# Weight sums through idle x places, and gate weights in 12 tiles per pair of blocks

## The chip, the cores and the metric

The kernel runs on one NeuronCore of a Trainium2 chip. A core has five engines with an instruction queue each: TensorE (PE; its weight loads are shown apart as PEld), VectorE (DVE), ScalarE (ACT), GpSimd (POOL) and SyncE (SP). SyncE issues nearly all loads, GpSimd nearly all stores; the transfers themselves run on 16 DMA engines. Every queue is worked off in order: an instruction that waits holds all those behind it. The metric is the time of one execution on the device in microseconds.

## The reference, cut to what matters

A decoder trunk of two layers over 2048 tokens of width 1024, fp32:

```python
# layer 0: x = x + mlstm_mixer(rmsnorm(x))
proj = u @ w_in                      # xm, z, o: 2048 columns each, and i, f: 4 each
xc = silu(causal_dwconv(xm))
q, k, v = per head from xc, xc, xm
h = chunkwise mLSTM, 64 tokens a chunk
y = (norm(sigmoid(o) * h) + skip * xc) * silu(z)
return y @ w_out                     # w_out: 2048 x 1024
# layer 1: x = x + rglru_mixer(rmsnorm(x))
proj = u @ w_in                      # xr, g: 1536 columns each
xc = causal_dwconv(xr)
xb = xc.reshape(bsz, s, 8, 192)      # 8 blocks of 192 channels
r  = sigmoid(xb @ w_a + b_a)         # per block 192 x 192
ig = sigmoid(xb @ w_x + b_x)
log_a = -8 * r * softplus(-lam)
bt = sqrt(-expm1(2 * log_a)) * (ig * xc)
hs = scan over tokens: h = exp(log_a) * h + bt
return (hs * silu(g)) @ w_out        # 1536 x 1024
# and a final rmsnorm
```

The two things the change touches are `y @ w_out` of layer 0 (its weights are prepared long before it is computed) and the two gate products `xb @ w_a`, `xb @ w_x` of layer 1.

## The kernel before, in words

Activations lie with channels on the 128 partitions and tokens along the free axis, in blocks of 512 tokens. Every fp32 product is made of three matmuls: each operand is split into a rounded high part (a ScalarE cast, L750) and the rest (a VectorE subtraction, L753), and `mm3` (L359 to L361) adds high × high, low × high and high × low into one PSUM bank. There are eight banks of 128 x 512.

**Phases.** a1: first norm and the projections xm, z, o; a2: chunkwise mLSTM; b: the output projection `y @ w_out`, second norm, the projections xr and g; b2: gates, scan, output projection of layer 1, final norm.

**Phase a1.** Large products go by a seven-product scheme on 2 x 2 quarters (a "group": seven products of 12 matmuls on sums of quarters, whose partial results pa, pb, pc, pd VectorE adds up at L271). Tokens are worked in two slabs of 1024, s = 0 and 1. In each slab come first six groups whose first product was made early (`first`, these are z outputs; "late groups" below), then 14 or so middle items: four "q" items (`o_group`, the o projection of a head; they begin with the copies `G<-oa`, L540) and the groups of the other outputs. Weights of a group stream from DRAM: in the second slab the raw quarters come over SyncE (L83, L424) and their stored sums come back into the s ring (`s<-d_wx`, L98).

**The weight sums of phase b.** `wout_sums(k)`, k = 0 to 7, loads four 128 x 512 pieces of w_out (L468) into four places of the x ring, makes four combinations in place (L471), splits each into a slot of the s ring of 128 x 1024 (cast `s<-x` L750, low part L753) and stores the slot with one DMA of 512 KB on GpSimd's queue (L93, `d_ws<-s`). Phase b reads these sums back. The program calls it at the first eight middle items of the second slab. The x ring has eight places, the s ring eight slots, which the streaming weights use too. The x ring held the input blocks of the first slab and is not otherwise used by the second slab's middle items.

**Phase b2.** For each block b of 512 tokens and each pair p = 0 to 3 of gate blocks (a pair is 384 channels, three partition tiles xc[0..2]) the generator `gates` runs in two halves. The weights of a pair are cut into 128 x 128 tiles: output tile 0 needs input tiles 0, 1; output tile 1, in which the border of the two blocks lies, needs 0, 1, 2; output tile 2 needs 1, 2: seven tiles for r and seven for ig. Half 0 makes r: tanh (L1425), exp to A (L1428), tanh to R (L1429), then one square root over all three tiles (L1433, which changes ScalarE's function table) and a VectorE product (L1436). Half 1 makes ig (tanh, L1431), then on VectorE the products (L1438, L1439), the scan (L1442), the product with silu(g) (L1445), and the split into yh and yl, which the matmuls `acc<-yh,wr` of the output projection need. The steps of gates ("g") and of the output projection ("r") are interleaved in `steps` with a lag of five, so that matmuls of one block's output projection lie between gate halves of the next.

**What sets the order.** The program text gives each instruction a place, but a list scheduler of the compiler decides the order on each engine from its own estimate of when operands and buffers are free; so instructions may move far ahead of the place of their call.

Of the kernel before, what the change touches and what calls it, by code (L numbers as in the profile page):

```python
# [8 lines left out]
F32R = mybir.dt.float32r  # L9
I32 = mybir.dt.int32  # L10
AF = mybir.ActivationFunctionType
# [3 lines left out]
P = 128  # L15
# [291 lines left out]
class Trunk:  # L307
# [74 lines left out]
    def phase_a1(self, xT, woq, wxz, wout, D):  # L382
        tc, nc = self.tc, self.nc
        with ExitStack() as ctx:
# [77 lines left out]

            def wout_sums(k):

                A = {}
                for nm, kk, c in (("11", k, 0), ("21", k, 512), ("22", k + 8, 512), ("12", k + 8, 0)):
                    A[nm] = S.x()
                    nc.sync.dma_start(A[nm], wout[kk, :, c:c + 512])  # L468

                def comb(out, a, b, op):  # L470
                    nc.vector.tensor_tensor(A[out], A[a], A[b], op=op)  # L471
                comb("22", "21", "22", ALU.add)
                comb("21", "11", "21", ALU.subtract)
                comb("11", "22", "11", ALU.subtract)
                comb("12", "12", "11", ALU.subtract)
                for nm, i in (("22", 0), ("11", 1), ("21", 2), ("12", 3)):
                    S.split(A[nm], D["ws"][i, k])

# [133 lines left out]
            for k in range(KD):  # L612
                S.scale(xs, None, pb, (k,))
                nm = ("u11", "u21")[k // 4]
                U[nm, k % 4] = S.operand(nm, k % 4, xs[k], "v")
            ew = []
            for s in range(2):
                t = []
# [11 lines left out]
                for j, (kind, i) in enumerate(middle):  # L630
                    W = stream()
                    if s == 1 and j < 8:
                        wout_sums(j)
                    if kind == "q":
# [689 lines left out]
    def phase_b2(self, rgate, rwout, D, outT):  # L1324
# [4 lines left out]
        with ExitStack() as ctx:  # L1329
# [14 lines left out]
            def fetch(kind, b, i):  # L1344

                m = 896 if kind == "g" else 512
                pool = gp if kind == "g" else wp
                keep = D["gw" if kind == "g" else "ow"][i]
                if b > 0:
# [3 lines left out]
                raw = pool.tile([P, m], F32, tag="wr" + kind, name="wr", bufs=2)  # L1353
                nc.gpsimd.dma_start(raw, rgate[i // 2, :, i % 2 * 896:(i % 2 + 1) * 896] if kind == "g" else
                                    rwout[i % NT, :, i // NT * 512:(i // NT + 1) * 512])
# [52 lines left out]
            def gates(b, p, xs, ys):  # L1408
# [4 lines left out]
                xc, xh, xl = xs  # L1413
                for j in range(2):
                    wh, wl = weights()
                    i = 0
                    for to, tis in ((0, (0, 1)), (1, (0, 1, 2)), (2, (1, 2))):
                        ps = psum("gate")
                        for ti in tis:
                            ws = slice(i * P, (i + 1) * P)  # L1420
                            self.mm3(ps, wh[:, ws], wl[:, ws], xh[:, ti], xl[:, ti], ti == tis[0], ti == tis[-1])
                            i += 1
                        t = p * 3 + to
                        if j == 0:
                            a = nc.scalar.activation(R[:, to], ps, AF.Tanh, scale=0.5, bias=col(2, t))  # L1425
                            if b == 0 and t == 5:
                                self.first.append(a)
                            nc.scalar.activation(A[:, to], R[:, to], AF.Exp, scale=col(0, t), bias=col(0, t))  # L1428
                            nc.scalar.activation(R[:, to], R[:, to], AF.Tanh, scale=col(1, t), bias=col(1, t))  # L1429
                        else:  # L1430
                            nc.scalar.activation(G[:, to], ps, AF.Tanh, scale=0.5, bias=col(3, t))  # L1431
                    if j == 0:
                        nc.scalar.activation(R, R, AF.Sqrt, scale=-0.25)  # L1433
                        g = tp.tile([P, 3, TB], F32, tag="g", name="g")
                        nc.sync.dma_start(g, D["g"][p * 3:p * 3 + 3, :, b * TB:(b + 1) * TB].rearrange("k p t -> p k t"))
                        nc.vector.scalar_tensor_tensor(R, A, 1.0, R, op0=ALU.add, op1=ALU.mult)  # L1436
                        yield
                nc.vector.scalar_tensor_tensor(xc, G, 1.0, xc, op0=ALU.add, op1=ALU.mult)  # L1438
# [94 lines left out]
def host(inputs):  # L1533
# [36 lines left out]
    o["rwout"] = np.ascontiguousarray(f["r_w_out"][0].reshape(12, P, DM))  # L1570
    rg = np.zeros((4, P, 14, P), np.float32)
    for p in range(4):
        i = 0
        for nm in ("r_w_a", "r_w_x"):
            m = np.zeros((384, 384), np.float32)
            m[:192, :192] = f[nm][0][2 * p]
            m[192:, 192:] = f[nm][0][2 * p + 1]
            for to, tis in ((0, (0, 1)), (1, (0, 1, 2)), (2, (1, 2))):
                for ti in tis:
                    rg[p, :, i] = m[ti * P:(ti + 1) * P, to * P:(to + 1) * P]  # L1580
                    i += 1
    o["rgate"] = rg.reshape(4, P, 1792)
    o["gbias"] = np.stack([np.repeat(f["m_b_i"][0], 16), np.repeat(f["m_b_f"][0], 16)], axis=1)
# [3 lines left out]
def trunk_kernel(tc, xT, woq, wxz, wq, wk, wv, wout, rwin, rgate, rwout, vecs, gbias, outT):  # L1587
    with ExitStack() as ctx:
        K = Trunk(ctx, tc, vecs, gbias)
        D = {}  # L1590
        for n, shape in (("o", [NTC, P, MI]), ("xm", [16, P, T]), ("xc", [16, P, T]), ("sz", [16, P, T]),
                         ("y", [16, P, T]), ("x1", [KD, P, T]), ("xr", [12, P, T]), ("g", [12, P, T]), ("q", [64, P]), ("dec", [64, P]), ("wx", [16, 4, P, 1024]),
                         ("wq", [H, 4, 2, P, 1032]), ("wr", [12, 4, P, 1024]), ("ws", [4, 8, P, 1024]),
                         ("gw", [8, P, 1792]), ("ow", [24, P, 1024])):
            D[n] = tc.dram_tile(shape, F32, name="d_" + n)
# [28 lines left out]
```

## Time and profile before

| | us |
|---|---|
| median of three runs | 3014.07 (3010.29 to 3014.26) |
| profiled execution | 3012.88, span 3011.1, mean TensorE clock 0.983 |
| TensorE busy | 2886.6 (96%) |
| VectorE, ScalarE, GpSimd busy | 2128.8, 1496.0, 433.1 |

The late groups of the second slab lie at 548 to 632 us, its middle items with the weight sums at 632 to about 900, phase b2 from about 2520 to the end. The page gives sums over the whole span; for what one change is worth, the windows and waits of its own stage are read. In a row of a timeline the first number is the start, the second the duration, and a bracket at the end names the idle time ahead of it and who ended it. In a row of a tile the three numbers behind the count are the shortest, median and longest duration in ns (for DMA issues: the issue alone), then the first and last start; "landing" is the time from issue to arrival.

### The profile page before, as it was taken

The page shows a single profiled execution, that of the slowest core. Times are in us where ns is not written, and L with a number is a line of the kernel's source. Part 1 is how long each engine was busy: PE and PEld are TensorE (multiplying, and loading weights), DVE is VectorE, ACT ScalarE, POOL GpSimd, SP SyncE. Part 2 cuts the span into 40 slices and gives each one's busy share as a digit, 9 for nine tenths or more (in the row PEclk, how much of TensorE's full clock was granted, in tenths as well). Part 3 has the DMA queues.
Part 4 walks back from the last instruction along what each step waited for, and adds up shares of the span by engine and source line. Part 5 has one row for each costly group of instructions (what it writes and reads, how often), then busy time and mean ns, then how long its engine had stood idle before and what let it go on. Part 6 is the DMA issues. An engine that isn't in the chain of part 4 may idle for free. (4 is left out here: it accounts for less than half of the span.)

```text
span 3011.1 us, 43310 instructions
## 1 busy us (share of the span) xinstructions
PE 2886.6 (96%) x15538; PEld 2469.6 (82%) x15538; DVE 2128.8 (71%) x3596; ACT 1496.0 (50%) x2526; POOL 433.1 (14%) x838
## 2 busy tenths in 40 slices
PE   7999999999899999999999899999999998899997
PEld 5799987898887799998999777887888886687886
DVE  7766788535567588788888756768889475766654
ACT  6344555324334466666666433435445235865651
POOL 1211132101112111111111201002221111110000
PEclk9999999999999999999999999999999998999998
DMA  6767677768887745444443667676766657878865
GB/s 227 266 220 252 229 250 244 244 206 293 282 275 262 224 138 168 130 147 153 146 146 121 246 220 269 217 246 219 244 230 212 217 177 279 297 268 291 295 201 185
DMA packets 289272, 672.43 MB, mean 223 GB/s; under 512 B 28064, under 2 KB 106656, under 8 KB 289056
## 3 DMA queue, kind: packets, MB, share of 16 engines
q1 hardware_dynamic: 219952, 425.17, 44.7%
q0 software_dynamic: 68528, 243.44, 21.2%
q8 instruction: 122, 2.00, 0.3%
q10 hardware_dynamic: 576, 1.05, 0.1%
q14 instruction: 94, 0.77, 0.1%
HBM read 431.33 MB, written 238.22 MB: 222 GB/s over the span
## 5 line engine op out<-in xcount | busy, mean ns | idle before, releaser
L750 ACT CAST s<-raw 128x512 fp32r<-128x512 f32 (+1 forms) x280 | 171.6, 620 | 246.3 <-PE pd L361 71.5
L753 DVE TENSOR_TENSOR s<-raw,s 128x512 fp32r<-128x512 f32 (+1 forms) x280 | 191.7, 689 | 69.3 <-ACT s L750 68.2
L359 PE MATMUL acc<-yh,wr 128*128 128x512 f32 x384 | 153.7, 407 | 17.4 <-ACT yh L750 11.4
L360 PE MATMUL acc<-yl,wr 128*128 128x512 f32 x384 | 155.1, 404 | 1.7 <-DVE yl L753 1.7
L361 PE MATMUL acc<-yh,wr 128*128 128x512 f32 x384 | 154.4, 402 | 0.0
L750 ACT CAST u<-t 128x512 fp32r<-128x512 f32 x112 | 68.8, 619 | 153.1 <-PE pc L361 50.3
L677 DVE SCALAR_TENSOR_TENSOR xc<-xm,vec,xc 128x512 f32<-128x512 f32 x192 | 139.4, 747 | 5.4 <-ACT xc L675 4.2
L753 DVE TENSOR_TENSOR u<-t,u 128x512 fp32r<-128x512 f32 x112 | 76.8, 690 | 84.2 <-ACT u L750 83.8
L750 ACT CAST s<-sum 128x512 fp32r<-128x512 f32 (+1 forms) x120 | 74.0, 618 | 116.8 <-PE pc L361 46.5
L359 PE MATMUL pa<-u,s 128*128 128x512 f32 x304 | 122.5, 403 | 4.6 <-ACT p L258 3.1
L360 PE MATMUL pa<-u,s 128*128 128x512 f32 x304 | 121.6, 400 | 0.0
L361 PE MATMUL pa<-u,s 128*128 128x512 f32 x304 | 121.4, 400 | 0.1
L750 ACT CAST Ch<-C 128x516 fp32r<-128x516 f32 x120 | 74.8, 623 | 85.4 <-DVE da L980 70.3
L962 DVE SCALAR_TENSOR_TENSOR C<-C,dl,kv 128x516 f32<-128x516 f32 x112 | 83.7, 747 | 47.2 <-PE kv L361 47.2
L677 DVE SCALAR_TENSOR_TENSOR xc<-xr,vec,xc 128x512 f32<-128x512 f32 x144 | 106.0, 748 | 9.2 <-ACT xc L675 8.1
L359 PEld LDWEIGHTS acc<-yh,wr 128*128 128x128 f32 x384 | 73.7, 193 | 38.9 <-ACT yh L750 13.6
L359 PE MATMUL pj<-vwh,xmh 128*128 128x512 f32 x256 | 102.7, 402 | 0.7 <-ACT vwh L750 0.7
L360 PE MATMUL pj<-vwl,xmh 128*128 128x512 f32 x256 | 99.9, 390 | 0.8 <-DVE vwl L753 0.8
L753 DVE TENSOR_TENSOR s<-sum,s 128x512 fp32r<-128x512 f32 (+1 forms) x120 | 82.7, 690 | 24.9 <-ACT s L750 24.1
L361 PE MATMUL pj<-vwh,xml 128*128 128x512 f32 x256 | 100.2, 391 | 0.0
L359 PE MATMUL gate<-xch,wg 128*128 128x512 f32 x224 | 90.6, 406 | 9.4 <-ACT xch L750 9.3
L360 PEld LDWEIGHTS acc<-yl,wr 128*128 128x128 f32 x384 | 74.3, 193 | 20.8 <-DVE yl L753 3.4
(481 smaller groups left out, 10090.9 us busy)
## 6 DMA issues: line engine op xcount, KB each, us to landing
wr<-d_ow SPq DMA_DIRECT2D x72, 512.0 KB, 3.7
d_wx<-s POOLq DMA_DIRECT2D x64, 512.0 KB, 4.3
s<-d_wx SPq DMA_DIRECT2D x64, 512.0 KB, 4.8
s<-d_ws SPq DMA_DIRECT2D x64, 512.0 KB, 6.5
raw<-in_wxz_dram SPq DMA_DIRECT2D x124, 256.0 KB, 4.7
d_wr<-s POOLq DMA_DIRECT2D x48, 512.0 KB, 3.7
s<-d_wr SPq DMA_DIRECT2D x48, 512.0 KB, 4.2
raw<-in_rwin_dram SPq DMA_DIRECT2D x94, 256.0 KB, 3.8
```

The source lines that it names most:

```text
L359: mm(out, sh, mh, start=first, stop=False, skip_group_check=resumed)
L360: mm(out, sh, ml, start=False, stop=False, skip_group_check=resumed)
L361: mm(out, sl, mh, start=False, stop=last, skip_group_check=resumed)
L677: nc.vector.scalar_tensor_tensor(out, x[:, j:j + TB], self.v(wn, m * 4 + j), out, op0=ALU.mult, op1=ALU.add)
L750: a = nc.scalar.copy(hi, src)
L753: b = (nc.gpsimd if lo_eng == "p" else nc.vector).tensor_tensor(lo, src, hi.bitcast(F32), op=ALU.subtract)
L962: nc.vector.scalar_tensor_tensor(C2, C2, self.dl[:, r:r + 1], p2, op0=ALU.mult, op1=ALU.add)
```

## The change

It has two parts.

**Weight sums.** `wout_sums` is cut in two: `wout_blocks(k)` takes four x places and loads the pieces; `wout_sums(k, A)` makes the same combinations, takes a further x place for the high part of each and leaves the low part in place, and stores the two parts with a DMA of 256 KB each. No s slot is used. The calls stand at the middle items 0, 2, 3, 5, 7, 8, 10, 11, and a sum is made one item behind its loads.

**Gates.** For output tile 1 the program now packs columns: its first 64 columns belong to the first block of the pair and need input tiles 0, 1; its last 64 belong to the second and need 1, 2. The bank "low" holds 64 columns of r and 64 of ig over tiles 0, 1, and "high" the same over tiles 1, 2, with the halves swapped. So a pair has six output banks of two tiles each, 12 tiles, in place of six banks of 2, 3 and 2. Half 0 makes r0, low and high, half 1 makes r2, i0 and i2; the activations of the shared banks work on 64 partitions each (four in place of two), and the square root with its product stands in half 1, since r2 is made there. The weights of one half are 768 columns wide (896 before).

```diff
-            def wout_sums(k):
+            def wout_blocks(k):
 
                 A = {}
                 for nm, kk, c in (("11", k, 0), ("21", k, 512), ("22", k + 8, 512), ("12", k + 8, 0)):
                     A[nm] = S.x()
                     nc.sync.dma_start(A[nm], wout[kk, :, c:c + 512])
+                return A
+
+            def wout_sums(k, A):
 
                 def comb(out, a, b, op):
                     nc.vector.tensor_tensor(A[out], A[a], A[b], op=op)
...
                 for nm, i in (("22", 0), ("11", 1), ("21", 2), ("12", 3)):
-                    S.split(A[nm], D["ws"][i, k])
+                    hi, lo = S.x(), A[nm]
+                    self.split_into(hi.bitcast(F32R), lo.bitcast(F32R), lo, "a", "v")
+                    nc.gpsimd.dma_start(D["ws"][i, k, :, 0:TB], hi)
+                    nc.gpsimd.dma_start(D["ws"][i, k, :, TB:2 * TB], lo)
...
+            spread, sums = (0, 2, 3, 5, 7, 8, 10, 11), []
...
                     W = stream()
-                    if s == 1 and j < 8:
-                        wout_sums(j)
+                    if sums:
+                        wout_sums(*sums.pop())
+                    if s == 1 and j in spread:
+                        sums.append((spread.index(j), wout_blocks(spread.index(j))))
...
-                m = 896 if kind == "g" else 512
+                m = 768 if kind == "g" else 512
...
-                for j in range(2):
+                def banks(what):
                     wh, wl = weights()
                     i = 0
-                    for to, tis in ((0, (0, 1)), (1, (0, 1, 2)), (2, (1, 2))):
+                    for nm, tis in what:
                         ps = psum("gate")
                         for ti in tis:
                             ws = slice(i * P, (i + 1) * P)
                             self.mm3(ps, wh[:, ws], wl[:, ws], xh[:, ti], xl[:, ti], ti == tis[0], ti == tis[-1])
                             i += 1
-                        t = p * 3 + to
-                        if j == 0:
-                            a = nc.scalar.activation(R[:, to], ps, AF.Tanh, scale=0.5, bias=col(2, t))
...
-                            nc.scalar.activation(A[:, to], R[:, to], AF.Exp, scale=col(0, t), bias=col(0, t))
-                            nc.scalar.activation(R[:, to], R[:, to], AF.Tanh, scale=col(1, t), bias=col(1, t))
-                        else:
-                            nc.scalar.activation(G[:, to], ps, AF.Tanh, scale=0.5, bias=col(3, t))
-                    if j == 0:
+                        yield nm, ps
...
+                for nm, ps in banks((("r0", (0, 1)), ("low", (0, 1)), ("high", (1, 2)))):
+                    if nm == "r0":
+                        rec(0, ps, every)
+                        rates(0)
+                    elif nm == "low":
+                        rec(1, ps, low)
+                        inp(1, ps, low, high)
+                    else:
+                        rec(1, ps, high)
+                        inp(1, ps, high, low)
+                        rates(1)
+                yield
+                for nm, ps in banks((("r2", (1, 2)), ("i0", (0, 1)), ("i2", (1, 2)))):
+                    if nm == "r2":
+                        a = rec(2, ps, every)
...
+                        rates(2)
                         nc.scalar.activation(R, R, AF.Sqrt, scale=-0.25)
                         g = tp.tile([P, 3, TB], F32, tag="g", name="g")
                         nc.sync.dma_start(g, D["g"][p * 3:p * 3 + 3, :, b * TB:(b + 1) * TB].rearrange("k p t -> p k t"))
                         nc.vector.scalar_tensor_tensor(R, A, 1.0, R, op0=ALU.add, op1=ALU.mult)
-                        yield
+                    else:
+                        inp(int(nm[1]), ps, every, every)
```

Lines of the changed program have other numbers: the combinations are L474 (L471 before), splits L759 and L762 (L750, L753), the half stores L482 and L483, the square root L1463 (L1433), tanh of r L1435 (L1425), tanh of ig L1438 (L1431), exp and tanh of the rates L1442 and L1443 (L1428, L1429).

VectorE, phase a1, second slab, at the end of the first late group and through the second (z, u and p are the groups' work tiles, pb to pd their PSUM banks, raw and s the streamed weights). Before:

```order
L271 TENSOR_TENSOR z<-pd,u_5638 128x512
L271 TENSOR_TENSOR u_5729<-pb,p_5300 128x512
L753 TENSOR_TENSOR s<-raw,s 128x512
L271 TENSOR_TENSOR p_5300<-pc,u_5729 128x512
L271 TENSOR_TENSOR z<-pd,p_5300 128x512
L271 TENSOR_TENSOR z<-pc,u_5729 128x512
L271 TENSOR_TENSOR z<-pd,u_5729 128x512
```

and after:

```order
L271 TENSOR_TENSOR z<-pd,u_5638 128x512
L474 TENSOR_TENSOR x<-x 128x512 x2
L271 TENSOR_TENSOR u_5729<-pb,p_5300 128x512
L762 TENSOR_TENSOR s<-raw,s 128x512
L474 TENSOR_TENSOR x<-x 128x512 x2
L271 TENSOR_TENSOR p_5300<-pc,u_5729 128x512
L762 TENSOR_TENSOR x<-x 128x512 x3
L271 TENSOR_TENSOR z<-pd,p_5300 128x512
L762 TENSOR_TENSOR x<-x 128x512
L271 TENSOR_TENSOR z<-pc,u_5729 128x512
L474 TENSOR_TENSOR x<-x 128x512
L271 TENSOR_TENSOR z<-pd,u_5729 128x512
```

Sum 1 now stands in the second late group. It is so in all six: of the eight sums all 32 combinations and low parts stand ahead of the first `G<-oa` of the middle items, the last two combinations of sum 7 just behind and the two before them just ahead of the last addition of the sixth group. Before, only the combinations of sums 0 and 1 stood there.

SyncE, the same groups. Before:

```order
L98 DMA s<-d_wx 128x1024 x3
L424 DMA raw<-in_woq_dram 128x516
L98 DMA s<-d_wx 128x1024 x4
L424 DMA raw<-in_woq_dram 128x516
L98 DMA s<-d_wx 128x1024 x4
L83 DMA raw<-in_wxz_dram 128x512
```

and after:

```order
L98 DMA s<-d_wx 128x1024
L468 DMA x<-in_wout_dram 128x512
L98 DMA s<-d_wx 128x1024
L468 DMA x<-in_wout_dram 128x512 x2
L98 DMA s<-d_wx 128x1024
L468 DMA x<-in_wout_dram 128x512
L98 DMA s<-d_wx 128x1024
L468 DMA x<-in_wout_dram 128x512
L424 DMA raw<-in_woq_dram 128x516
L98 DMA s<-d_wx 128x1024
L468 DMA x<-in_wout_dram 128x512 x2
L98 DMA s<-d_wx 128x1024
```

Loads of w_out now stand between the loads of the stored weight sums; each of them takes an x place whose store must have landed.

ScalarE, phase b2, from the last rate steps of a pair to the cast of the next pair's input. Before:

```order
L1425 ACTIVATE R<-gate,lc 128x512
L1429 ACTIVATE R<-R,lc 128x512
L1428 ACTIVATE A<-R,lc 128x512
L1429 ACTIVATE R<-R,lc 128x512
L1433 ACT_TABLE_LOAD
L1433 ACTIVATE R<-R 128x1536
L1511 COPY rb<-srow 128x512
L1431 ACT_TABLE_LOAD
L1431 ACTIVATE ig<-gate,lc 128x512 x3
L750 CAST xch<-xc 128x1536
```

and after:

```order
L1435 ACTIVATE R<-gate,lc 128x512
L1442 ACTIVATE A<-R,lc 128x512
L1438 ACTIVATE ig<-gate,lc 128x512
L1443 ACTIVATE R<-R,lc 128x512
L1438 ACTIVATE ig<-gate,lc 128x512
L1463 ACT_TABLE_LOAD
L1463 ACTIVATE R<-R 128x1536
L759 CAST xch<-xc 128x1536
L1435 ACT_TABLE_LOAD
```

The square root has moved behind the last tanh of ig. On TensorE the matmuls between the last gate matmul of pair 3 and the first output matmul on that pair's yh number 64 between blocks (57 before), as ten gate matmuls of the next block's second half are drawn ahead, and 37 behind the last block (36 before). The gate matmuls are 576 in all (672 before).

More of the change, by code (lines that the diff above doesn't have):

```diff
@@ L1353, in fetch @@
                 raw = pool.tile([P, m], F32, tag="wr" + kind, name="wr", bufs=2)
-                nc.gpsimd.dma_start(raw, rgate[i // 2, :, i % 2 * 896:(i % 2 + 1) * 896] if kind == "g" else
+                nc.gpsimd.dma_start(raw, rgate[i // 2, :, i % 2 * 768:(i % 2 + 1) * 768] if kind == "g" else
                                     rwout[i % NT, :, i // NT * 512:(i // NT + 1) * 512])
@@ L1422, in gates, with rec, inp, rates @@
                             i += 1
-                        t = p * 3 + to
-                        if j == 0:
[L1425 to L1428, printed above, removed]
-                            nc.scalar.activation(R[:, to], R[:, to], AF.Tanh, scale=col(1, t), bias=col(1, t))
-                        else:
-                            nc.scalar.activation(G[:, to], ps, AF.Tanh, scale=0.5, bias=col(3, t))
-                    if j == 0:
+                        yield nm, ps
+                def rec(to, ps, rows):
+                    return nc.scalar.activation(R[rows, to], ps[rows], AF.Tanh, scale=0.5, bias=col(2, p * 3 + to)[rows])
+                def inp(to, ps, rows, src):
+                    nc.scalar.activation(G[rows, to], ps[src], AF.Tanh, scale=0.5, bias=col(3, p * 3 + to)[rows])
+                def rates(to):
+                    t = p * 3 + to
+                    nc.scalar.activation(A[:, to], R[:, to], AF.Exp, scale=col(0, t), bias=col(0, t))
+                    nc.scalar.activation(R[:, to], R[:, to], AF.Tanh, scale=col(1, t), bias=col(1, t))
+                every, low, high = slice(0, P), slice(0, 64), slice(64, P)
+                for nm, ps in banks((("r0", (0, 1)), ("low", (0, 1)), ("high", (1, 2)))):
[13 more added lines that the diff above has]
+                        a = rec(2, ps, every)
+                        if b == 0 and p == 1:
+                            self.first.append(a)
+                        rates(2)
                         nc.scalar.activation(R, R, AF.Sqrt, scale=-0.25)
@@ L1570, in host @@
     o["rwout"] = np.ascontiguousarray(f["r_w_out"][0].reshape(12, P, DM))
-    rg = np.zeros((4, P, 14, P), np.float32)
+    rg = np.zeros((4, P, 12, P), np.float32)
     for p in range(4):
-        i = 0
[L1574 to L1582, printed above, removed]
+        m = []
+        for nm in ("r_w_a", "r_w_x"):
+            m.append(np.zeros((384, 384), np.float32))
+            m[-1][:192, :192] = f[nm][0][2 * p]
+            m[-1][192:, 192:] = f[nm][0][2 * p + 1]
+        r, x = m
+        low = np.concatenate([r[:, 128:192], x[:, 128:192]], axis=1)
+        high = np.concatenate([x[:, 192:256], r[:, 192:256]], axis=1)
+        i = 0
+        for w, tis in ((r[:, 0:128], (0, 1)), (low, (0, 1)), (high, (1, 2)), (r[:, 256:384], (1, 2)),
+                       (x[:, 0:128], (0, 1)), (x[:, 256:384], (1, 2))):
+            for ti in tis:
+                rg[p, :, i] = w[ti * P:(ti + 1) * P]
+                i += 1
+    o["rgate"] = rg.reshape(4, P, 1536)
     o["gbias"] = np.stack([np.repeat(f["m_b_i"][0], 16), np.repeat(f["m_b_f"][0], 16)], axis=1)
@@ L1593, in trunk_kernel @@
                          ("wq", [H, 4, 2, P, 1032]), ("wr", [12, 4, P, 1024]), ("ws", [4, 8, P, 1024]),
-                         ("gw", [8, P, 1792]), ("ow", [24, P, 1024])):
+                         ("gw", [8, P, 1536]), ("ow", [24, P, 1024])):
             D[n] = tc.dram_tile(shape, F32, name="d_" + n)
```

## The prediction

> **What bounds the kernel now.** I read the page first, then stage by stage the table of windows, and after it the waits, tiles and timelines of the two places the change touches.
>
> ```profile
> span 3011.1 us, 43310 instructions
> PE 2886.6 (96%) x15538; PEld 2469.6 (82%) x15538; DVE 2128.8 (71%) x3596; ACT 1496.0 (50%) x2526; POOL 433.1 (14%) x838
> ```
>
> TensorE is busy for 96% of the span: 124.5 us of 3011.1 are idle. A change gains by taking matmuls away where TensorE is the bound, or by closing one of its gaps; it loses wherever it makes a new one. The columns of the next view are the window, its length, the busy time of TensorE, weight loads, VectorE, ScalarE and GpSimd with their instruction counts, the granted clock, the DMA share and GB/s.
>
> ```profile
> core 0: us, PE busy (x) PEld busy (x) DVE busy (x) ACT busy (x) POOL busy (x), PEclk, DMA share, GB/s
> 150.00:310.00 160.00, 160.00 (x1168) 152.00 (x1167) 107.23 (x239) 76.31 (x143) 27.32 (x51) 1.00 0.66 231
> 548.00:632.00 84.00, 84.00 (x364) 67.94 (x363) 34.61 (x53) 17.94 (x29) 10.25 (x19) 1.00 0.74 241
> 690.00:900.00 210.00, 193.70 (x1289) 176.54 (x1290) 122.20 (x273) 81.96 (x153) 27.89 (x52) 0.98 0.84 285
> 2520.00:2627.00 107.00, 86.57 (x327) 66.21 (x327) 75.39 (x63) 89.41 (x114) 24.15 (x45) 0.89 0.92 332
> 2627.00:2740.00 113.00, 109.58 (x459) 88.07 (x460) 77.77 (x72) 69.01 (x90) 16.12 (x29) 0.96 0.81 287
> 2860.00:2900.00 40.00, 40.00 (x174) 32.52 (x173) 25.27 (x17) 20.60 (x26) 0.00 (x0) 1.00 0.63 211
> ```
>
> Rows 1 and 3 hold the same kind of work, the middle items of phase a1, without and with the weight sums. With them TensorE is idle for 210.00 − 193.70 = 16.3 us and the clock is 0.98; without them it has neither. Row 2 is the stretch just ahead, the six late groups of the second slab: no idle at all. Row 4 is block 0 of the gate phase, with 20.4 us of idle; row 6 a steady piece of it, full, where 40.00 / 174 = 0.230 us is the price of one 512-column matmul.
>
> **The middle items, 690 to 900 us.** The sums are removed from here: the order of VectorE puts all eight ahead of the first middle item, although the program text spreads their calls. The waits of TensorE here (us in all, times, longest) and what the sums do:
>
> ```profile
> PE pd L359 <- DVE xm L271: 7.2, 3, 3.3
> PE st L714 <- DVE gate L709: 2.6, 1, 2.6
> PE st L694 <- DVE G L540: 1.1, 1, 1.1
> ```
> ```profile
> L468 SPq DMA_DIRECT2D x<-in_wout_dram x32: 327/333/1185, 543.2 to 872.1; - x32
> L471 DVE TENSOR_TENSOR x<-x x32: 681/687/695, 553.0 to 877.9; 128x512 f32<-128x512 f32 x32
> L750 ACT CAST s<-x x32: 601/620/622, 672.3 to 903.5; 128x512 fp32r<-128x512 f32 x32
> L753 DVE TENSOR_TENSOR s<-x,s x32: 620/692/694, 672.9 to 904.2; 128x512 fp32r<-128x512 f32 x32
> DMA to landing us min/median/max: 3.1/5.3/7.4
> ```
>
> The longest waits are for VectorE, whose queue holds sums that themselves wait for loads. What can go is the 16.3 us of idle and the lost clock, 0.02 × 210 = 4.2 us: 20.5 in all. The two gate steps (2.6 + 1.1 us) have nothing to do with the sums. I take **−16** (bounds −20.5, and −12 if some clock loss stays). Row 1 is the cover: the same items ran there with no gap.
>
> **The late groups, 548 to 632 us.** What left the middle arrives here. Before, only the combinations of sums 0 and 1 stood here; now all 32 combinations, 32 casts on ScalarE, 32 low parts on VectorE, and 64 stores of 256 KB on GpSimd's queue (32 of 512 KB before), whose issues are short. The engines have room: 24 × 0.687 + 32 × 0.692 = 38.6 us more on VectorE, beside 34.6 busy of 84. The question is the wait. A sum takes four x places for its blocks and four for the high parts, all eight of the ring, so the loads of the next sum wait until the stores of this one have landed; and the additions of the groups (L271) stand behind the combinations in VectorE's queue, TensorE's PSUM banks behind those additions, and the next groups' weight loads (s<-d_wx) behind the waiting x loads in SyncE's queue. The prices:
>
> ```profile
> 553.02 1.41 DVE L471 TENSOR_TENSOR x<-x 128x512 f32<-128x512 f32 x2
> 559.20 2.13 DVE L471 TENSOR_TENSOR x<-x 128x512 f32<-128x512 f32 x3
> 632.05 0.69 DVE L271 TENSOR_TENSOR z<-pd,u 128x512 f32<-128x512 f32 x1 [2.10 <-PE pd L361]
> 639.27 0.16 DVE L540 COPY G<-oa 128x2 f32<-128x2 f32 x1
> ```
> ```profile
> GB/s 193 238 125 198 339 218 198 294 390 402 358 243 221 0 81 94 239 153 254 322 340 398 279 239 190 301 209 193 269 235 174 249 277 175 120 202 197 207 299 54
> s<-d_wx SPq DMA_DIRECT2D x24, 512.0 KB, 4.2
> d_sz<-z POOLq DMA_DIRECT2D x32, 256.0 KB, 4.0
> x<-in_wout_dram SPq DMA_DIRECT2D x8, 256.0 KB, 6.1
> ```
> ```profile
> d_ws<-s POOLq DMA_DIRECT2D x29, 512.0 KB, 5.5
> ```
> ```profile
> L93 POOL DMA_DIRECT2D d_ws<-s x32: 531/532/539, 673.9 to 905.2; - x32
> DMA to landing us min/median/max: 2.9/6.1/10.9
> ```
>
> One round: three combinations 2.1 (the x3 row), two casts 1.2, the store's issue 0.5 and landing 4.0 (d_sz, the same size, 460 to 640 us) to 5.5 (d_ws, 640 to 900 us), the next load's issue 0.3 and landing 5.3: C = 13.4 to 14.9 us. Sum 0 starts at 553.0 as before; the combinations of sum 7 stand ahead of the last addition of group 6, which therefore can't come before 553.0 + 7C = 647 to 657 instead of 632.05: +15 to +25. With the shortest landings of the rows, 2.9 and 3.1, C is 10.1 and nothing is lost. With 6.1 for both landings (the whole d_ws tile and the x loads of this stretch) C is 16.3: +35.
>
> A second way, by bytes: the stretch moves 241 × 84 = 20.2 MB; eight sums are 64 × 256 KB of stores and 32 × 256 KB of loads, 25.2 MB, of which eight loads (2.1) were there already: 43.3 MB. At 402 GB/s, the fullest slice of the DMA view (460 to 640 us), that is 107.7 us, or 97.3 if the last two sums' stores (4.2 MB) land later: +13 to +24. At what row 4 of the windows would make of a full share, 332 / 0.92 = 361 GB/s, it is 108 to 120 us: +24 to +36. Both ways meet between 15 and 25; I take **+22**, bounds 0 and +36.
>
> The Trainium skill, page "DMA: Bandwidth & Descriptors", section "Anatomy of one DMA — SWDGE (gpsimd) path", prices a store as about 2.0 us plus its bytes at 436 GB/s; for 256 KB that is an estimate of 2.6 us, and with it for both landings a round would take 9.3 us and the sums would keep pace (rival 2). The rows above, 4.0 to 6.1 us, are longer, so I go by them. The same page's section "Where 436 GB/s comes from" sets about 358 GB/s as a core's share of HBM; that speaks against this change and would put the loss at +25 to +37, though the 402 of one slice shows that this rate is passed at times.
>
> **The gates (phase b2).** Each pair of blocks drops 2 of 14 tiles: 2 × 3 matmuls, 96 over 16 pairs. Each pair gains two ScalarE activations, since the shared banks are read by halves of 64 rows.
>
> ```profile
> L1425 ACT ACTIVATE R<-gate,lc x48: 663/672/695, 2527.0 to 2926.0; 128x512 f32<-128x512 f32 x48
> L1431 ACT ACTIVATE ig<-gate,lc x48: 667/687/691, 2538.0 to 2939.3; 128x512 f32<-128x512 f32 x48
> L701 ACT ACTIVATE gate<-gate x1: 312/312/312, 873.7 to 873.7; 64x128 f32<-64x128 f32 x1
> ```
> ```profile
> PE acc L359 <- ACT yh L750: 11.4, 4, 3.3
> ```
>
> An activation on 64 rows of 512 columns isn't in the trace. A 64x128 one took 0.312; four times the columns cost at most 4 × 0.312 = 1.25 and at least that 0.31. I take 0.67, the same columns on twice the rows: 32 × 0.67 = 21.4 us more on ScalarE (10 to 40). In blocks 1 to 3 this lies beside matmuls: ScalarE is busy 69.01 of 113 in row 5 and 20.60 of 40 in row 6.
>
> Blocks 1 to 3 lose 72 matmuls: 72 × 0.230 = −16.6, as TensorE is nearly full there. In block 0 ScalarE is busy 89.41 of 107 us and TensorE isn't the bound: 24 matmuls could give −5.5, eight more activations could cost +5.4; I take 0.
>
> The square root (L1433, with its table load) and the product behind it move from the first half of a pair to the second, so they come after the last gate matmul:
>
> ```profile
> 2823.57 1.76 DVE L1436 SCALAR_TENSOR_TENSOR R<-A,R 128x1536 f32<-128x1536 f32 x1 [6.57 <-ACT R L1433]
> 2834.94 1.75 DVE L1439 TENSOR_TENSOR R<-R,xc 128x1536 f32<-128x1536 f32 x1
> 2836.73 3.63 DVE L1442 TENSOR_TENSOR_SCAN xc<-A,hcarry,R 128x512 f32<-128x512 f32 x3
> 2840.40 1.76 DVE L1445 TENSOR_TENSOR g<-xc,g 128x1536 f32<-128x1536 f32 x1
> ```
> ```profile
> 2820.76 1.28 ACT L1433 ACT_TABLE_LOAD   x1
> 2822.05 1.49 ACT L1433 ACTIVATE R<-R 128x1536 f32<-128x1536 f32 x1
> 2842.19 1.48 ACT L750 CAST yh<-g 128x1536 fp32r<-128x1536 f32 x1 [1.01 <-DVE g L1445]
> ```
> ```profile
> L1428 ACT ACTIVATE A<-R,lc 128x512 f32<-128x512 f32 x5 | 4.0, 805 | 0.0
> ```
>
> From the last gate matmul to yh it is now tanh 0.69, table 1.28, root 1.49, product 1.76, product 1.75, scan 3.63, product 1.76 and cast 1.48: 13.8 us. The cover between blocks is 64 matmuls in the changed order (57 before), 64 × 0.230 = 14.7 us: just enough, so 0 there. Behind the last pair of block 3 only 37 matmuls stand, 8.5 us: a wait of 5.3 instead of the longest in the row above, 3.3: +2 (0 to +4). Gates: −16.6 + 0 + 2 = **−15** (bounds −22, all 96 matmuls and no new wait, and −4, worked out as rival 3).
>
> **Sum.** −16 + 22 − 15 = −9 us against the profiled execution's 3012.88 us, 3004; the median shown is 1.2 us above that execution, so 3005.
>
> **Rivals.**
> 1. *The loads hold the weights (slower).* SyncE works in order: an x load that waits for a landed store holds the weight loads behind it, and those arrive 4.2 us after issue, longer than one product of twelve matmuls, 12 × 0.230 = 2.8 us. If the two waits add up in each round, C = 14.2 + 2.8 to 4.2 = 17.0 to 18.4, the last addition comes at 672 to 682 and the late groups lose 40 to 50 us. With 45 the sum is +14: 3028. For it: two queues in order that wait on each other, and 43.3 MB in 84 us, 515 GB/s, above every slice. Against it: eight weight slots hold more than one product ahead. It decides from 31 us (C = 15.7), where the gains of the other two parts are used up.
> 2. *The sums keep pace.* Landings near 3 us: late groups 0 to +8, in all −27: 2987. For it: half-size stores, and single landings of 2.9 and 3.1 us. Against it: those are minima.
> 3. *The gate chain has no cover.* If two ScalarE steps of the next pair (0.805 each, the L1428 row) come between root and cast, the chain is 15.4 against 14.7 us and 0.7 is lost at each of 16 pairs, 11 in all; gates −4, sum +2: 3016, no change. For it: the chain has 0.9 us to spare, and ScalarE's queue is in order. Against it: in row 6 ScalarE is busy only half the time.
> 4. *It doesn't do what it says.* The order already shows the sums not spread over twelve items; the price is in the main case.
>
> **How the numbers follow.** Main case 0.45, rival 1 0.20, rival 2 0.20, rival 3 0.15. About 0.2% (6 us: below 3008.0, above 3020.1) is what can be told from no change here. Faster: two thirds of the main case and rival 2, 0.50. Slower: rival 1 with small tails of the main case and rival 3, 0.24. Same: the rest, 0.26. The range reaches from rival 2 to rival 1, 2984 to 3029, and leaves out about 0.2; the main case alone, with its late groups at +15 to +30, spans 2998 to 3013.
>
> **What would show it.** In the profile after: the stretch from 548 us to the first G<-oa copy (639.27 before) longer by some 22 us, with TensorE waiting for L271 additions that wait for L474, and DMA above 350 GB/s there; the middle items without the 16 us of idle; gate matmuls 576 instead of 672; TensorE's wait for yh at the end longer by about 2 us. I am wrong if the late groups stay without idle (rival 2), if their wait is for s<-d_wx rather than for additions (rival 1), or if waits for yh appear at each pair (rival 3).

## The result, and the profile after

The changed kernel takes 3033.86 us (median of four, 3029.15 to 3039.57) against 3014.0 before (median of four, too): 1.007 times, 95% interval 1.0051 to 1.0089. It is slower by about 20 us; the forecast was 3005, range 2984 to 3029. The profiled execution is the longest of the four, 3039.57 us, span 3037.8, so the differences between its trace and the one before add up to 26.7 us (span 3037.8 against 3011.1).

The head of the page after, and its windows over the late groups and the middle items (columns as in the prediction; the last row runs from the first sum to the first `G<-oa`):

```profile
span 3037.8 us, 43242 instructions
```
```profile
548.00:632.00 84.00, 62.68 (x239) 48.93 (x238) 42.21 (x69) 21.29 (x38) 25.36 (x48) 0.89 0.90 310
632.00:690.00 58.00, 41.22 (x189) 34.16 (x188) 27.43 (x44) 16.88 (x31) 17.97 (x34) 0.88 0.83 293
690.00:900.00 210.00, 210.00 (x1511) 198.82 (x1511) 96.37 (x213) 74.60 (x142) 14.55 (x28) 1.00 0.70 222
553.00:691.00 138.00, 99.91 (x409) 80.02 (x408) 65.69 (x105) 36.38 (x65) 43.25 (x81) 0.88 0.87 302
```

The middle items (690 to 900) are now full, 210.00 of 210.00 at clock 1.00. The late groups, full before, stand idle for 21.3 of their first 84 us and go on until 691: 38.1 us of 138 are idle. The waits there, of TensorE, VectorE and SyncE's queue in this order:

```profile
PE pc L359 <- DVE p L271: 28.6, 5, 7.5
PE oa L359 <- ACT p L554: 6.5, 1, 6.5
PE pd L359 <- DVE z L271: 3.1, 1, 3.1
```
```profile
DVE x L474 <- DMA x<-in_wout_dram: 62.2, 7, 12.9
```
```profile
SPq L468 <- DMA d_ws<-x: 61.5, 19, 11.6
```

This is a chain through three engines: the loads of w_out wait 61.5 us for stores of the sum ahead, the combinations (L474) wait 62.2 us for the loads, and TensorE waits for additions (L271) that stand behind the combinations. VectorE's timeline gives the rounds and the end:

```profile
553.59 1.41 DVE L474 TENSOR_TENSOR x<-x 128x512 f32<-128x512 f32 x2
573.61 1.42 DVE L474 TENSOR_TENSOR x<-x 128x512 f32<-128x512 f32 x2 [10.05 <-DMA x<-in_wout_dram]
...
684.16 1.42 DVE L474 TENSOR_TENSOR x<-x 128x512 f32<-128x512 f32 x2 [11.30 <-DMA x<-in_wout_dram]
685.50 0.68 DVE L271 TENSOR_TENSOR z<-pd,u 128x512 f32<-128x512 f32 x1
...
691.05 0.15 DVE L546 COPY G<-oa 128x2 f32<-128x2 f32 x1
```

The eight sums begin at 553.59 to 684.16: seven rounds of 18.65 us. The last z addition comes at 685.50 (632.05 before), the first copy of the middle items at 691.05 (639.27 before): **+51.8 us**. From that copy to the first gate matmul it takes 1859.4 us against 1884.1, **−24.8**; from the first gate matmul to the end 487.4 against 487.7, **−0.3**. The sum is +26.7. Of the −24.8, 20.0 us lie between that copy and the gate step behind it on TensorE (L694 at 872.34 before, L703 at 904.10 after), and 5.9 in the groups between this step and phase a2 (145.2 us before, 139.3 after); 1.1 is lost again later.

The DMA view from 553 to 690 us (KB each, median us to landing) and the landings of the x tile:

```profile
d_ws<-x POOLq DMA_DIRECT2D x61, 256.0 KB, 5.7
s<-d_wx SPq DMA_DIRECT2D x17, 512.0 KB, 9.0
x<-in_wout_dram SPq DMA_DIRECT2D x28, 256.0 KB, 8.6
```
```profile
DMA to landing us min/median/max: 2.3/6.6/12.4
```

The same 256 KB land after 2.3 us when they are the first of a burst and after up to 12.4 when they come late in it; a load of w_out takes 8.6 at the median where the forecast had 5.3.

Phase b2, cut at the first use of each block's last pair (block 0, then the boundaries to the next). Before, and then after:

```profile
2523.40:2620.90 97.50, 83.87 (x318) 64.84 (x319) 69.19 (x59) 79.94 (x102) 21.46 (x40) 0.89 0.92 336
2620.90:2733.30 112.40, 106.44 (x452) 85.04 (x450) 79.44 (x73) 68.43 (x88) 17.19 (x31) 0.97 0.80 283
2733.30:2843.70 110.40, 109.47 (x472) 88.53 (x472) 70.95 (x60) 66.49 (x82) 5.42 (x9) 0.98 0.81 277
2843.70:2950.90 107.20, 103.05 (x451) 83.51 (x451) 67.79 (x58) 63.29 (x78) 5.40 (x9) 1.00 0.71 239
```
```profile
2550.40:2662.50 112.10, 80.48 (x271) 59.83 (x272) 72.93 (x59) 83.47 (x107) 22.93 (x43) 0.82 0.81 289
2662.50:2768.30 105.80, 104.11 (x458) 84.52 (x456) 75.62 (x70) 77.64 (x101) 17.08 (x29) 1.00 0.79 282
2768.30:2871.40 103.10, 102.17 (x449) 82.86 (x449) 71.04 (x61) 72.09 (x90) 6.31 (x9) 1.00 0.81 289
2871.40:2976.00 104.60, 95.73 (x420) 77.60 (x420) 69.52 (x59) 65.90 (x83) 6.92 (x9) 0.98 0.70 245
```

The second to fourth stretch are shorter by 6.6, 7.3 and 2.6 us; the first is longer by 14.6 with 47 matmuls fewer in it (24 of them gone with the tiles, the rest now later), TensorE idle for 31.6 us in place of 13.6 and its clock 0.82 in place of 0.89. Not all of this idle time is a wait for ScalarE. One row of TensorE's waits in the first stretch, before and then after, is for VectorE:

```profile
PE gate L360 <- DVE xcl L753: 0.9, 1, 0.9
```
```profile
PE gate L360 <- DVE xcl L762: 6.8, 2, 6.2
```

The 6.2 us lie at 2650.8 to 2657.0. The subtraction that makes xcl stands in VectorE's queue behind the products and the scan of the pair before, which wait for that pair's square root and its last tanh.

The end of block 3 waits 8.9 us (TensorE's waits, and below them a group of the gate tile):

```profile
PE acc L359 <- DMA wr<-d_ow: 8.9, 1, 8.9
```
```profile
L1435 ACT ACTIVATE R<-gate,lc x64: 663/684/691, 2554.1 to 2956.1; 128x512 f32<-128x512 f32 x32, 64x512 f32<-64x512 f32 x32
```

The yh of the last pair is ready 5.7 us after TensorE fell idle (the cast ends at 2972.85); the last 3.2 us are for the weight load. The second row answers an open price: an activation on 64 partitions takes as long as one on 128 (0.680 us at the mean, and 0.683 on 128).

### The profile page after: what moved, and what is told of

Same layout as the page of the kernel before. It is cut to its first block, busy times and chain, and to the rows that moved or that the text cites. A ratio compares the mean times of both kernels' runs of the same rounds, so it can differ in the third digit from the quotient of the medians.

```text
span 3037.8 us, 43242 instructions
## 1 busy us (share of the span) xinstructions
PE 2874.6 (95%) x15442; PEld 2460.0 (81%) x15442; DVE 2130.9 (70%) x3596; ACT 1517.5 (50%) x2557; POOL 453.6 (15%) x870
## 5 line engine op out<-in xcount | busy, mean ns | idle before, releaser
L759 ACT CAST s<-raw 128x512 fp32r<-128x512 f32 (+1 forms) x280 | 172.2, 621 | 267.2 <-PE pc L361 69.1
L762 DVE TENSOR_TENSOR s<-raw,s 128x512 fp32r<-128x512 f32 (+1 forms) x280 | 191.2, 688 | 53.7 <-ACT s L759 52.5
L759 ACT CAST u<-t 128x512 fp32r<-128x512 f32 x112 | 68.8, 619 | 154.8 <-PE pc L361 51.0
L762 DVE TENSOR_TENSOR u<-t,u 128x512 fp32r<-128x512 f32 x112 | 76.7, 689 | 85.2 <-ACT u L759 84.9
L759 ACT CAST s<-sum 128x512 fp32r<-128x512 f32 (+1 forms) x120 | 74.0, 618 | 116.0 <-PE pc L361 46.4
L759 ACT CAST Ch<-C 128x516 fp32r<-128x516 f32 x120 | 74.8, 623 | 84.5 <-DVE da L989 69.8
L359 PEld LDWEIGHTS acc<-yh,wr 128*128 128x128 f32 x384 | 74.4, 195 | 43.3 <-issue 9.3
L762 DVE TENSOR_TENSOR s<-sum,s 128x512 fp32r<-128x512 f32 (+1 forms) x120 | 82.5, 688 | 25.2 <-ACT s L759 24.5
L359 PE MATMUL gate<-xch,wg 128*128 128x512 f32 x192 | 78.4, 412 | 16.9 <-ACT xch L759 11.7
```

The lines of the kernel that those rows point to most:

```text
L359: mm(out, sh, mh, start=first, stop=False, skip_group_check=resumed)
L759: a = nc.scalar.copy(hi, src)
L762: b = (nc.gpsimd if lo_eng == "p" else nc.vector).tensor_tensor(lo, src, hi.bitcast(F32), op=ALU.subtract)
```

## The experiments

Theory A: the two parts are independent; the weight sums lose because the order puts them all into the late groups. Rivals: the gates gain their 15 us and the sums lose 35; or the sums are slow wherever they stand. Ratios are against the kernel before, on the same chip.

### Each part alone

The first takes only the pieces of the diff in phase b2 and in the layout of the gate weights, the second only those in phase a1:

```diff
 e1_gates
-                m = 896 if kind == "g" else 512
+                m = 768 if kind == "g" else 512
...
 e2_sums
-                    S.split(A[nm], D["ws"][i, k])
+                    hi, lo = S.x(), A[nm]
...
```

> The kernel before with the gate part alone (12 tiles a pair); the weight sums as they were. In the trace of the whole change phase b2, from the first gate matmul to the end of the span, took 487.4 us against 487.7 before, although 96 matmuls (22.1 us) are gone. Theory A: the gates gain nothing by themselves, because block 0 gives back some 14 us in waits of TensorE for ScalarE: 3011 to 3016 us, TensorE idle in block 0 about 14 us more than before. Rival: the gates do bring the forecast 15 us and what hid it was a chance of that one profile (a slow stretch of the clock): 2997 to 3003 us.

> The kernel before with the weight-sum part alone; the gates as they were. The order puts all eight sums into the late groups here too. Theory A (the parts add, and the gates bring nothing): the first copy of the middle items at about 691 us instead of 639, the middle items 20 us shorter, in all 3034 us (3029 to 3040). Rival (the gates bring 15 us and the sums cost 35): 3045 to 3052 us.

Gates alone: 3005.81 us, 0.9985 (0.9975 to 0.9994). The kernel before took 3009.7 us on that chip. Sums alone: 3033.81, 1.008 (1.0065 to 1.0095); first copy of the middle items at 686.0. So the sums lose about 24 us, as theory A had it, and the gates gain about 4 (1.007 for both): the parts add up. The gates lie between the two expectations: a gain that can just be told, not 15 us.

### The sums held at their items

```diff
-                comb("22", "21", "22", ALU.add)
+                self.order((self.anchor,), (comb("22", "21", "22", ALU.add),))
```

`anchor` is the last addition of the item ahead (a group's or the o projection's), and `order` puts the combination behind it on VectorE; nothing else changes.

> The weight-sum part alone, with the first combination of each sum ordered behind the last group addition (or o-projection addition) of the item ahead of its call, so that the sums stand on VectorE where the program text has them, at the middle items 1, 3, 4, 6, 8, 9, 11, 12. Theory A (the loss is that the sums stand in the late groups): late groups without idle, first copy of the middle items back at 639 us, middle items shorter by 16 to 20 us as in the whole change, 2994 to 2999 us. Rival (x places and half stores are slow wherever they stand): the middle items get waits for x loads, 3010 us or more.

2988.22 us, 0.9936 (0.9919 to 0.9952): 21 us faster than before, a little more than the 16 to 20 expected, and 46 faster than the same code without the line. The first copy of the middle items is back at 638.4 us. Late groups and middle items of this run:

```profile
548.00:632.00 84.00, 84.00 (x368) 68.16 (x367) 29.67 (x45) 17.27 (x29) 10.22 (x19) 1.00 0.71 227
690.00:900.00 210.00, 209.19 (x1390) 191.55 (x1389) 131.46 (x300) 89.21 (x161) 35.74 (x68) 1.00 0.84 283
```

Both are full, at the same 283 GB/s over the middle items as before the change (285). With the same places, the same half stores and the same loads the run is now faster than before, so the place of the sums in VectorE's queue decided the sign. The rival falls.

### Fewer bytes in the late groups

```diff
-                    nc.gpsimd.dma_start(D["ws"][i, k, :, TB:2 * TB], lo)
```

> The weight-sum part alone, hoisted as in the change, but the low parts are neither made nor stored, and phase b reads the high part in their place (so the output projection of layer 0 is computed without them, and only the stretch from 553 us to the first copy of the middle items is read). In the whole change a round from sum to sum took 18.65 us and moved 5.6 MB at 302 GB/s. Theory B (bytes: the DMA engines are full): a round moves 1.05 MB less, 15.2 us at the same rate, and the first copy comes at about 553.6 + 7 x 15.2 + 7 = 667 us. Theory T (the round trip through eight places: a sum waits for its predecessor's stores to land): four places are free at once, the next loads start behind the casts, a round is below the groups' 13.9 us, and the copy comes at 639 to 645 us. If the store traffic doesn't matter at all: 691 us as before.

The low parts were made after all (their subtractions are in the trace), only their stores are gone. The first copy comes at 660.8 us; a round takes (652.36 − 552.98) / 7 = 14.2 us. The stretch from the first sum to that copy, and its DMA issues:

```profile
553.00:661.00 108.00, 92.00 (x405) 73.70 (x404) 64.59 (x105) 36.66 (x65) 26.85 (x50) 0.96 0.89 317
```
```profile
d_ws<-x POOLq DMA_DIRECT2D x32, 256.0 KB, 5.1
x<-in_wout_dram SPq DMA_DIRECT2D x28, 256.0 KB, 6.8
```

The waits of VectorE and of SyncE's queue in this stretch (62.2 and 61.5 in the whole change):

```profile
DVE x L474 <- DMA x<-in_wout_dram: 36.9, 9, 7.0
SPq L468 <- DMA d_ws<-x: 5.9, 3, 2.9
```

Theory B said 667 and 15.2, theory T 639 to 645 and below 13.9. The copy is 6 us from B and 16 from T; the round lies between them. The edit takes away stores and waits at once: four places come free when the low part is made, and the loads hardly wait for landed stores any more. Yet the copy is still 21.5 us later than before the change, so those waits are not all of the loss. The stretch moves 317 GB/s at a DMA share of 0.89, as the change does 302 at 0.87: divided out, 356 and 347 GB/s. The Trainium skill's page "DMA: Bandwidth & Descriptors", section "Where 436 GB/s comes from", sets about 358 GB/s as a core's share of HBM; the two quotients lie near it, while single slices of the DMA view pass it (419 in the change), so no run here shows it as a limit. The rate speaks for theory B, but one run that changes bytes and waits together can't part them: how much the bytes bear and how much the eight places isn't settled.

### Both parts, sums held

The whole change, with the edit of e3_held:

```diff
+                self.order((self.anchor,), (comb("22", "21", "22", ALU.add),))
```

> The whole change, with the sums held at their items as in the run that held the weight sums alone (that one measured 0.9936 of the kernel before), and the gates in 12 tiles (alone 0.9985). If the two parts don't touch each other: 0.9936 x 0.9985 = 0.992, about 2986 us. If the gates' part behaves otherwise behind a shorter phase a1: 2980 or 2990 us and beyond.

2984.94 us, 0.9921 (0.9905 to 0.9938): the product of the parts, 0.992.

### What block 0 of the gates lost

Theory W: casts of gate weights that wait at the head of ScalarE's queue. In the first stretch of phase b2 of the gates alone, and before:

```profile
ACT wg L750 <- DMA d_gw<-wg: 11.3, 2, 7.2
```
```profile
ACT wg L750 <- DMA d_gw<-wg: 6.6, 3, 3.4
```

Theory L: the late square root, which now stands behind a pair's last gate matmuls. Three places for gate weights (e6_ring3) test W, r2 in the first half (e7_early) tests L, and e8_held_early is e7_early with the sums held:

```diff
 e6_ring3
-                both = pool.tile([P, 2 * m], F32R, tag="w" + kind, name="w" + kind)
+                both = pool.tile([P, 2 * m], F32R, tag="w" + kind, name="w" + kind, bufs=4 if kind == "r" else 3)
 e7_early
-                for nm, ps in banks((("r0", (0, 1)), ("low", (0, 1)), ("high", (1, 2)))):
+                for nm, ps in banks((("r0", (0, 1)), ("low", (0, 1)), ("high", (1, 2)), ("r2", (1, 2)))):
...
-                for nm, ps in banks((("r2", (1, 2)), ("i0", (0, 1)), ("i2", (1, 2)))):
+                for nm, ps in banks((("i0", (0, 1)), ("i2", (1, 2)))):
```

> The gate part alone with three places for the gate weights in place of two (and one place for the squares of the final norm in place of two, to make room). In block 0 ScalarE stood 11.3 us, twice, at the cast of a gate weight whose place waited for its store to land, with the input cast that TensorE waits for (8.3 us) behind it. Theory W (that wait is what block 0 lost): it is gone, TensorE idle in block 0 falls from 36 us to about 25, in all some 8 to 10 us below the gate part alone (which was 3006): 2996 to 2998 us. Theory L (the late square root and the longer chain of each pair is what block 0 lost): 3004 to 3007 us.

> The gate part alone with r2 in the first half of a pair (8 tiles in the first half, 4 in the second), so that the square root and its product stand in the first half as in the kernel before; the weight tiles are the same (squares of the final norm in one place, as in the run beside it). Theory L (the late square root): TensorE idle in block 0 back near the 21 us of the kernel before, the wait at the end of block 3 back near 3.3 us (8.2 with the gate part alone), in all 12 to 18 us below the gate part alone: 2988 to 2994 us. Theory W (the casts that wait for stores): 3002 to 3007 us, since the weights still have two places.

> The sums held at their items together with the gates whose square root stands in the first half. Theory L: 0.9936 times what the early square root alone brings, 2968 to 2974 us. Theory W: 2984 us.

e6_ring3 took 3007.12 us (0.9986, 0.9977 to 0.9995) and e7_early 3006.19 (0.9987, 0.9977 to 0.9996): neither differs from the gates alone. With three places the casts no longer wait for stores, and the first stretch is 106.3 us in place of 112.5. But the free place lets a third weight cast stand ahead of the first input cast, where it waits 5.2 us for its load, and TensorE's wait at the start of phase b2 grows from 4.3 to 8.8 us: most of what the stretch gains goes there. With the early root TensorE's wait for xcl is gone, but one of 6.8 us for yh stands where the second stretch begins: the first takes 100.6 us, the second 116.1, together 216.7 against 217.9. The last wait is 5.8 us, for yh. With the sums held, the early root gives 2986.25 (0.9923, 0.9909 to 0.9938), as without it. Neither theory is the whole cause: each edit takes its wait away, and the time goes elsewhere.

Then ScalarE's queue itself: the eight casts moved to VectorE, with 12 tiles and with 14 (sums held in both), and the kernel before with the added activations alone:

```diff
 e10_vcast, e11_vcast14
-                a = self.split_into(both[:, 0:m], both[:, m:2 * m], raw, "a", "v")
+                a = self.split_into(both[:, 0:m], both[:, m:2 * m], raw, "v" if kind == "g" else "a", "v")
 e12_halves (and the same for G)
-                            a = nc.scalar.activation(R[:, to], ps, AF.Tanh, scale=0.5, bias=col(2, t))
+                            for h in (slice(0, 64), slice(64, P)) if to == 1 else (slice(0, P),):
+                                a = nc.scalar.activation(R[h, to], ps[h], AF.Tanh, scale=0.5, bias=col(2, t)[h])
```

> The sums held at their items and the gates in 12 tiles, with the casts of the eight gate weights of block 0 on VectorE in place of ScalarE, where they waited for stores and loads (11.3 us) at the head of the queue. Without this edit 2984.94 us (0.9921). Block 0 up to the first use of its last pair takes 112 us with the 12 tiles and 97.5 before. Theory A (ScalarE's queue in order is what block 0 lost): the stretch falls to about 100 us, 2973 us in all. Rival (the loss is in the order of the matmuls and the PSUM banks, not in ScalarE): the stretch stays at 108 to 114 us, 2983 to 2988 us.

> The same move of the eight casts with the gates as before (14 tiles) and the sums held (2988.22 us without the move, 0.9936). Theory A: block 0 takes 98.5 us here and has only 6.6 us of such waits, so 2982 to 2986 us. If moving the casts helps just as much with 14 tiles (10 us or more), then it isn't what the 12 tiles lost.

> The kernel before, with each tanh of output tile 1 made in two halves of 64 partitions (32 more activations of about 0.68 us, as the 12 tiles need) and nothing else: 14 tiles, square root in the first half. Theory A2 (the longer ScalarE work alone is what block 0 lost): block 0 up to the first use of its last pair 105 to 112 us in place of 97.5, in all 8 to 15 us more than before, 3020 to 3027 us. Rival (it is the moved chain and the order, not the number of activations): within 4 us of before.

e10_vcast took 2980.71 us (0.9902, 0.9884 to 0.992), e11_vcast14 2988.05 (0.9923, 0.9903 to 0.9942) and e12_halves 3016.22 (1.0019, 1.0009 to 1.003). The intervals of e10_vcast and of the same code without the move (0.9905 to 0.9938) overlap, and so do those of e11_vcast14 and e3_held, so the traces have to tell. The first stretch of phase b2 in e10_vcast, and in e12_halves:

```profile
2503.40:2606.20 102.80, 75.42 (x271) 56.52 (x272) 75.45 (x65) 79.19 (x101) 22.15 (x41) 0.84 0.83 296
```
```profile
2521.20:2628.40 107.20, 85.66 (x317) 65.38 (x318) 71.77 (x61) 88.09 (x112) 22.52 (x42) 0.87 0.85 312
```

Moving the casts shortens the stretch by 9.4 us with 12 tiles (112.2 to 102.8) and by 2.7 with 14 (98.5 to 95.8). But it also delays the first gate matmul. With 12 tiles, without the move and with it:

```profile
2496.73 0.80 PE L360 MATMUL gate<-xch,wg 128*128 128x512 f32 x1 [4.48 <-ACT xch L761]
```
```profile
2503.41 0.80 PE L360 MATMUL gate<-xch,wg 128*128 128x512 f32 x1 [10.14 <-ACT xch L761]
```

With 14 tiles this wait grows from 5.08 to 8.93 us. Wait and stretch together are 116.7 us with 12 tiles and 103.6 with 14; with the casts moved they are 112.9 and 104.7. So the move gains 3.8 us with 12 tiles and loses 1.1 with 14: of the 13.1 us between them the casts on ScalarE explain some 4 to 5, not most. The stretch (102.8) missed the 100 us of theory A by little, and the total lies between the two forecasts; e11_vcast14 lies above its own (2982 to 2986).

The added activations alone lengthen the stretch from 97.5 to 107.2 us, as expected, out of the 15.0 us that the gates alone lose there (112.5). In all they cost 1.0019, some 6 us, which is less than expected, since the next stretch gives 5.9 back. So the added activations on ScalarE are the largest part of block 0's loss that a run shows by itself, and the casts that wait in the same queue a smaller one. The wait of TensorE for VectorE's xcl is still 7.0 us in e10_vcast. That these parts add up was not shown, and what else keeps TensorE idle for 27.4 of 102.8 us in e10_vcast stays open.

Of the 10.1 us by which phase b2 became shorter in e10_vcast, 6.7 went at its start, where the first two casts now stand on VectorE ahead of phase b's last addition. With those two left on ScalarE:

```diff
-                a = self.split_into(both[:, 0:m], both[:, m:2 * m], raw, "v" if kind == "g" else "a", "v")
+                a = self.split_into(both[:, 0:m], both[:, m:2 * m], raw, "v" if kind == "g" and i > 1 else "a", "v")
```

> As the run with the eight casts on VectorE, but the first two stay on ScalarE: in that run they stood on VectorE ahead of the last addition of phase b, waited there 8.35 us for their loads, and phase b2 began 6.7 us later than without the move, which used up most of the 10.1 us that phase b2 became shorter. Theory A (ScalarE's queue in order is what block 0 loses): phase b2 begins at about 2497 us again and keeps most of the 10 us, 2974 to 2978 us. If the first two casts were the ones that mattered: 2981 to 2985 us.

2979.01 us, 0.9889 (0.9872 to 0.9905), between the two forecasts. Phase b2 begins at 2494.9 after a wait of 4.48 us again, and takes 481.0 us (474.8 with all eight moved, 484.9 with none): the start is won back, and 3.9 of the 10.1 us are kept. The first stretch is 108.7 us, not 102.8. It is the fastest version measured, 34 us below the kernel before on the same chip (3012.85), though its interval overlaps that of e10_vcast.

## Why the prediction was wrong, point by point

- **Late groups, +22 forecast, +51.8 measured: the step that failed.** Its mechanism was there, in the place and order described: the loads wait for landed stores, the combinations for loads, TensorE for L271 behind them. Mis-sized were the terms of the round. It was put together from landings of stretches with room, 4.0 to 5.5 for a store and 5.3 for a load; packed together they took 5.7 and 8.6 at the median, and late in a burst up to 12.4, so C was 18.65 in place of 13.4 to 14.9. With these two medians the prediction's own sum gives 18.4. The estimate by bytes had the right quantity, some 42 MB (302 × 138), but divided it by the fullest slice (402 GB/s); the stretch sustained 302. The row that would have told was at hand: 332 GB/s was the highest mean of any window in the prediction's table, and 43.3 MB at that rate are 130 us, +46. The sign that was named, DMA above 350 GB/s there, didn't come.
- **Rival 1** had the right size (40 to 50 us, C 17.0 to 18.4) from a mechanism that didn't decide: s<-d_wx landed late (9.0), but TensorE's waits name the additions, not the weights. That its 3028 lies near the result is luck.
- **Middle items, −16 forecast, −24.8 measured** up to phase b2. Right in kind: idle 16.3 and lost clock went to nothing, and the 20.0 us won up to the gate step are nearly the bound of 20.5 that the forecast had for both, not the 16 it took. Of the gate steps left standing, the 2.6 us (L709) are gone in the trace after as well; that and the other time won behind the items was not tested by itself.
- **Gates, −15 forecast, −0.3 in this trace, 0.9985 alone (some 4 us).** Behind block 0 the forecast was −16.6 + 2 = −14.6 and the three stretches gave −16.5. That this fits is partly chance: e12_halves, with no matmul less, has its second stretch 5.9 us shorter too, and the end took 8.9 in place of 5.3, released by a late weight load (the chain to yh, 5.7, was priced well). Block 0, taken as 0 between −5.5 and +5.4, cost 14.6: the row said that ScalarE was busy for 89.41 of 107 us, and its 21.4 us of added work was priced rightly (0.68 each against 0.67), but for block 0 I counted the busy time of eight activations (5.4 us), not what they hold up in a queue in order: alone they lengthened the stretch by 9.7. The late root's chain was checked against its cover for yh, not for the xcl behind it in VectorE's queue (6.2 us).
- Rivals 2 and 3 and the doubt about twelve items: the sums didn't keep pace; waits for yh at each pair didn't appear; and the change indeed didn't do what its text says until the sums were held there.

## What to carry to other kernels

Work moved to an idle buffer can be hoisted by the scheduler as soon as the buffer lets it: look at the order, and tie the work to its place, since here one ordering line was worth 46 us. A third place for the gate weights did the same on a small scale: it let a cast move ahead of the input cast that TensorE waits for. A chain through a full DMA queue must be priced with the landings of its own burst: divide the bytes by the highest mean over a long window, not by the fullest slice. In block 0 fewer matmuls brought nothing, since TensorE waited there for queues of other engines, worked off in order; count there what each added instruction holds up. And when an edit shortens a stretch, look whether the stretch only begins later.

## What the runs showed of the hardware

An activation on 64 partitions of 512 columns takes 0.68 us, as one on 128 does. Stores and loads of 256 KB land after 2.3 to 12.4 us in one stretch, by their place in the burst. In block 0, more idle time of TensorE went with a lower granted clock (0.89 with 13.6 us idle, 0.82 with 31.6), and a matmul that remains there costs more as well: 271 took 80.48 us busy, 318 took 83.87 before.
